# Three feed-forwards of a two-layer encoder: their first hidden group as a fifth seven-product group, and some low parts formed by adding DMAs

## The chip, the core and the metric

The kernel runs on one core of a Trainium2 chip. The core has a matmul engine (TensorE; PE on the page, its weight loads PEld), VectorE (DVE), ScalarE (ACT), GpSimd (POOL) and SyncE (SP); the engines run side by side and meet through semaphores. Matmuls read SBUF and add into eight banks of PSUM. Weights come from HBM by DMA, issued here by SP (plain loads) or by POOL (loads that add to what stands in SBUF). The metric is the device time of one execution in microseconds (us). A difference of about 0.2% (4.3 us) can be told from none in this kernel.

## The reference

512 tokens of width 1024 pass through two layers; each has a half-weight SwiGLU feed-forward, a token mixer, a cross-attention into 256 memory tokens, and a second feed-forward, each with a residual and a layer norm. All is fp32.

```python
def swiglu(x, w_gate, w_up, w_down):
    return (jax.nn.silu(x @ w_gate) * (x @ w_up)) @ w_down
...
    for i in range(DEPTH):                       # DEPTH = 2
        y = swiglu(x, ffn_w_gate[i, 0], ffn_w_up[i, 0], ffn_w_down[i, 0])
        x = layer_norm(ALPHA * x + 0.5 * y, ln_g[i, 0], ln_b[i, 0])
        y = mixer_ab(...) if i % 2 == 0 else mixer_c(...)
        x = layer_norm(ALPHA * x + y, ln_g[i, 1], ln_b[i, 1])
        y = memory_attn(x, mem, mem_w_q[i], mem_w_kv[i], mem_w_o[i])
        x = layer_norm(ALPHA * x + y, ln_g[i, 2], ln_b[i, 2])
        y = swiglu(x, ffn_w_gate[i, 1], ffn_w_up[i, 1], ffn_w_down[i, 1])
        x = layer_norm(ALPHA * x + 0.5 * y, ln_g[i, 3], ln_b[i, 3])
```

So there are four feed-forwards; gate and up are 1024 x 2816, down is 2816 x 1024. "Feed-forwards 2 to 4" are the ones with i = 1, 2, 3 in the kernel's `ffn` (line 873); the second follows the first memory attention, the third follows the second directly, the fourth is the last stage.

## The kernel before

**Precision.** Each operand is split into a high part (the value rounded to the matmul's fp32r format) and a low part (the value minus its high part). A product takes three matmuls: high by high, high by low, low by high (`mm3`, line 375). ScalarE makes the high part by a cast, VectorE the low part by a subtraction (`split`, 364; `wide`, 642, for a weight block of 128 x 1024 elements).

**Tokens.** After a layer norm each block of 128 tokens is transposed (`to_features`, 475): `xh` and `xl` hold the high and low parts with features on the partitions, and, ahead of a feed-forward, two `raw` buffers keep the unsplit values (`xf`).

**A feed-forward's hidden features** come in five groups of 512 (each two column ranges of 256, the tuple `groups`, 878) and a rest of 256. Groups 1 to 4 are made by seven products in place of eight (`hidden_steps`, 690; `quarters`, 696): the token matrix and the weight are cut into 2 x 2 quarters, sums of quarters are multiplied, and the results are added in PSUM. The products are named 1 to 7 and run in the order 1, 6, 5, 2, 7, 4, 3 for gate and then for up. Products 1, 2 and 3 use token quarters as they are (1 and 2 those of the first 256 tokens); 6, 5, 7, 4 use sums of token quarters that `token_sums` (671) makes once per feed-forward. On the weight side 1, 2 and 4 use quarters as loaded (a, b, d), 6, 5, 7, 3 sums of them; one of these sums is finished by a DMA that adds a quarter from HBM into SBUF (`plus`, 647), issued by POOL. A product is 24 matmuls of 256 columns. Product 2 adds into the bank of 1, 7 and 4 into that of 6, 3 into that of 5.

**Group 0** in feed-forwards 2 to 4 is made in full: its first 256 features by `ffn_by_tokens` (616; token blocks stationary, gate and up side by side in 512 columns, then eight transposes), its second 256 by `hidden` (658; weights stationary, all 512 tokens moving): 96 matmuls of 512 columns each. The by-token part needs one token block at a time, so it starts while later blocks are still in their layer norm.

**Down products** of group g - 1 (`down_steps`, 766) are 14 steps of six matmuls of 512 columns; `ffn` lays them between the products of group g.

**Order.** `ffn` makes a list of steps, each with a load, a preparation and a product; `staged` (862) calls the load of step j, the preparation of step j - 2 and the product of step j - 3, which fixes the order in which work is recorded. A list scheduler (`plan`, 186) then goes over all recorded operations with costs per engine, gives out buffers in the order asked for (27 weight buffers `slab` of 128 x 1024 fp32, 14 `t2`, 8 PSUM banks), and fixes each engine's order. Engines keep that order: an instruction that waits holds up those behind it on its engine. POOL's queue holds the adding DMAs, the rsqrt of the layer norms (`lny`) and some additions to x.

## Time and profile before

| | |
|---|---|
| Median of 3 runs (lowest, highest) | 2127.75 us (2125.88, 2128.41) |
| Profiled execution | span 2123.9 us, first to last instruction; the page gives no other time of it, and the median lies 3.85 us above |
| TensorE busy, weight loads busy | 2109.2 us (99%), 1871.0 us (88%) |
| VectorE, ScalarE, GpSimd busy | 1735.8 (82%), 1161.2 (55%), 287.4 us (14%) |
| Granted TensorE clock | 0.998 |
| HBM read | 259.12 MB, 124 GB/s over the span |
| Adding DMAs on POOL for gate and up | 32 of 512 KB |
| Feed-forwards on the timeline | 0 to 325, 708 to 1050, 1055 to 1390, 1779 to 2124 us |

In a row of the page stand the engine, the operation, output <- inputs by the names in the program, partitions x elements, the count, then busy us and mean ns of one, then the idle time ahead of it and what ended that. Busy TensorE time is pipelined: a matmul's own duration is longer than its spacing from the next. A merged row of the timeline gives the start of its first instruction and the time to the end of its last.

### The profile page before, as it was taken

How to read it: one execution, taken by the hardware profiler on the slowest of the kernel's cores; microseconds unless marked ns; L12 is line 12 of the kernel's file. 1: busy time of each engine (PE TensorE's matmuls, PEld its weight loads, DVE VectorE, ACT ScalarE, POOL GpSimd, SP SyncE). 2: the span in 40 equal slices, each digit the busy share in tenths (PEclk: the TensorE clock that was granted, in tenths of full speed). 3: DMA queues.
4: the chain of work that ended last, by engine and by line, in shares of the span. 5: the costliest groups of instructions: out<-in, count | busy, mean ns of one | idle time of the engine just before them, and what ended most of it. 6: DMA issues, size and time to landing. Idle time of an engine off the chain costs nothing.

```text
span 2123.9 us, 32745 instructions
## 1 busy us (share of the span) xinstructions
PE 2109.2 (99%) x12648; PEld 1871.0 (88%) x12648; DVE 1735.8 (82%) x2500; ACT 1161.2 (55%) x1903; POOL 287.4 (14%) x379
## 2 busy tenths in 40 slices
PE   9999999999999999999999999999999999999997
PEld 7999988888888899998889999888888888999996
DVE  7789988888748879998879999866577479699997
ACT  5555443698546554545545455457764465444552
POOL 0001015310102000000200000312210021000003
PEclk9999999999999999999999999999999999999999
DMA  6566562004434346564445556356454433456551
GB/s 205 141 168 144 136 191 91 21 18 116 140 125 109 90 117 181 150 158 129 148 100 143 126 139 186 78 147 165 119 165 155 139 93 96 110 149 155 143 149 60
DMA packets 208860, 275.93 MB, mean 130 GB/s; under 512 B 10688, under 2 KB 151616, under 8 KB 208704
## 3 DMA queue, kind: packets, MB, share of 16 engines
q1 hardware_dynamic: 175904, 221.14, 34.0%
q0 software_dynamic: 32512, 52.44, 14.1%
q8 instruction: 100, 1.64, 0.3%
q14 instruction: 56, 0.46, 0.1%
q10 hardware_dynamic: 288, 0.26, 0.0%
HBM read 259.12 MB, written 4.19 MB: 124 GB/s over the span
## 4 chain that ended last, share of the span: by engine, by line
PE 96%; DVE 1%; ACT 1%; DMA 1%; issue 0%; SPq 0%; DVEq 0%; ACTq 0%
PE a L157 59%; PE d L157 23%; PE t L157 15%; DVE slab L157 1%; ACT t L157 1%; DMA slab<-t 1%; DVE x L157 0%; ACT slab L157 0%; SPq L157 0%; DVE t L157 0%; DMA raw<-x_t 0%; ACT xh L157 0%; DVE mn L157 0%; DVE xl L157 0%; DVEq L1662 0%
## 5 line engine op out<-in xcount | busy, mean ns | idle before, releaser
L157 DVE TENSOR_TENSOR slab<-slab,slab 128x1024 fp32r<-128x1024 f32 (+3 forms) x638 | 727.5, 1166 | 69.5 <-ACT slab L157 39.9
L157 ACT CAST slab<-slab 128x1024 fp32r<-128x1024 f32 (+2 forms) x498 | 472.7, 983 | 341.5 <-DVE slab L157 173.2
L157 PE MATMUL a<-slab,slab 128*128 128x256 f32 (+3 forms) x2320 | 567.2, 322 | 0.7 <-DMA slab<-t 0.4
L157 PE MATMUL a<-xh,slab 128*128 128x256 f32 (+2 forms) x2480 | 559.9, 315 | 0.3 <-ACT slab L157 0.3
L157 PE MATMUL d<-slab,slab 128*128 128x512 f32 (+2 forms) x1856 | 447.0, 381 | 0.0
L157 PEld LDWEIGHTS a<-xh,slab 128*128 128x128 f32 x2480 | 416.4, 190 | 33.7 <-ACT slab L157 1.0
L157 PEld LDWEIGHTS a<-slab,slab 128*128 128x128 f32 x2320 | 409.5, 190 | 38.8 <-ACT t L157 1.3
L157 PE MATMUL a<-xl,slab 128*128 128x256 f32 (+1 forms) x1240 | 389.7, 314 | 0.0
L157 PE MATMUL a<-raw,slab 128*128 128x256 f32 x2048 | 388.9, 283 | 0.1
L157 PEld LDWEIGHTS d<-slab,slab 128*128 128x128 f32 x1856 | 329.0, 189 | 55.9 <-issue 0.2
L157 PEld LDWEIGHTS a<-raw,slab 128*128 128x128 f32 x2048 | 327.9, 192 | 5.4 <-ACT slab L157 0.5
L157 PEld LDWEIGHTS a<-xl,slab 128*128 128x128 f32 x1240 | 236.0, 190 | 18.4 <-DVE xl L157 0.4
L157 PE MATMUL t<-slab,slab 128*128 128x512 f32 (+1 forms) x840 | 209.5, 389 | 0.0
L157 DVE TENSOR_TENSOR slab<-raw,slab 128x1024 fp32r<-128x1024 f32 (+2 forms) x140 | 160.2, 1160 | 18.6 <-ACT slab L157 18.4
L157 PEld LDWEIGHTS t<-slab,slab 128*128 128x128 f32 x840 | 149.9, 189 | 26.3
L157 DVE TENSOR_TENSOR slab<-t,slab 128x512 fp32r<-128x512 f32 (+2 forms) x223 | 137.6, 638 | 16.4 <-ACT slab L157 15.9
L157 ACT CAST slab<-t 128x512 fp32r<-128x512 f32 (+2 forms) x223 | 120.9, 566 | 40.7 <-DVE t L157 13.9
L157 ACT CAST slab<-raw 128x1024 fp32r<-128x1024 f32 (+1 forms) x132 | 124.3, 971 | 27.9 <-PE a L157 8.8
L157 DVE SCALAR_TENSOR_TENSOR x<-d,x 128x512 f32<-128x512 f32 x168 | 114.7, 685 | 25.3 <-PE d L157 24.4
L157 ACT COPY t<-a 128x512 f32<-128x512 f32 (+1 forms) x116 | 63.5, 550 | 130.4 <-PE a L157 77.2
L157 POOL DMA_DIRECT2D slab<-ffn_w_down x40 | 47.7, 1193 | 310.3 <-DVE slab L157 276.3
L157 ACT ACTIVATE t<-a 128x512 f32<-128x512 f32 (+3 forms) x65 | 36.3, 559 | 89.0 <-PE a L157 89.0
(126 smaller groups left out, 2167.2 us busy)
## 6 DMA issues: line engine op xcount, KB each, us to landing
slab<-ffn_w_gate SPq DMA_DIRECT2D x80, 512.0 KB
slab<-ffn_w_up SPq DMA_DIRECT2D x80, 512.0 KB
slab<-ffn_w_down SPq DMA_DIRECT2D x80, 512.0 KB
slab<-ffn_w_down POOLq DMA_DIRECT2D x40, 512.0 KB, 5.8
raw<-mem_w_kv SPq DMA_DIRECT2D x16, 1024.0 KB
slab<-t SPq DMA_DIRECT2D x96, 128.0 KB
slab<-ffn_w_gate POOLq DMA_DIRECT2D x16, 512.0 KB, 7.8
slab<-ffn_w_up POOLq DMA_DIRECT2D x16, 512.0 KB, 6.0
```

The lines of the kernel that those rows point to most:

```text
L157: op.call = lambda: fn(*args, **kw)
```

## The change

Six things, all in the feed-forward code:

- In feed-forwards 2 to 4 group 0 becomes a seven-product group like the others; `ffn_by_tokens` goes. The first feed-forward keeps its way of making group 0.
- Groups 0 and 1 of these feed-forwards open with products 1 and 2 of gate and up of both groups, eight products that need only the first 256 tokens. Group 0's other ten products follow with no down step between, then group 1's ten with group 0's down steps spread among them. Group 1's products 1 use PSUM tag `d`, and its quarter a is loaded a second time for the later products.
- Low parts of the plain weight quarters that are not needed whole elsewhere go another way (`wide_late`): ScalarE copies the high part negated, and a DMA on POOL adds the weight from HBM. That is done for quarters b and d (products 2 and 4) in all 19 groups of all feed-forwards, and for a, b and d (1, 2, 4) in the two opening groups. (19 = 4 in the first, 5 in each other.)
- In the other groups quarter b's load and preparation stand at product 5 instead of 2, and quarter d's preparation at product 2 instead of 4.
- `token_sums` works in halves of the tokens, sums first and then splits; in feed-forwards 2 to 4 it is called at the preparation of group 0's product 6 instead of ahead of all groups.
- Some buffers are asked for later (`c22` at product 5, `h` one at a time).

By count, over the whole program: TensorE loses 576 matmuls of 512 columns and 24 transposes and gains 1008 matmuls of 256 columns. VectorE loses 72 operations of 128 x 1024 and gains some 64 of 128 x 512. ScalarE gains 88 negated copies and 14 casts of 128 x 1024, and 24 copies of 128 x 512. POOL gains 94 adding DMAs of 512 KB; SP issues 24 fewer loads of 256 KB and 18 more of 512 KB.

TensorE at the start of the second feed-forward, around the transposes of the last token block (`x3`; `t_` are PSUM banks, `a_1421` and `a_1425` banks of hidden features, `xh`, `xl` the tokens, `slab_` weight parts). Before:

```order
L157 MATMUL a_1421_1502<-slab_1416_1497,xl_3_84 128x512
L157 MATMUL a_1421_1502<-slab_1419_1500,xh_2_83 128x512
L157 MATMUL a_1421_1502<-slab_1420_1501,xh_2_83 128x512
L157 MATMUL t_1407_1488<-ident_1_78,x3_7_88 128x128 x4
L157 MATMUL a_1421_1502<-slab_1419_1500,xl_3_84 128x512
L157 MATMUL t_1408_1489<-ident_1_78,x3_7_88 128x128 x4
L157 MATMUL a_1421_1502<-slab_1419_1500,xh_2_83 128x512
L157 MATMUL a_1421_1502<-slab_1420_1501,xh_2_83 128x512
L157 MATMUL a_1421_1502<-slab_1419_1500,xl_3_84 128x512
```

Now:

```order
L157 MATMUL a_1425_1506<-xh_2_83,slab_1418_1499 128x256
L157 MATMUL a_1425_1506<-xh_2_83,slab_1417_1498 128x256
L157 MATMUL a_1425_1506<-xl_3_84,slab_1417_1498 128x256
L157 MATMUL t_1407_1488<-ident_1_78,x3_7_88 128x128 x4
L157 MATMUL a_1425_1506<-xh_2_83,slab_1418_1499 128x256
L157 MATMUL a_1425_1506<-xh_2_83,slab_1417_1498 128x256
L157 MATMUL t_1408_1489<-ident_1_78,x3_7_88 128x128 x4
L157 MATMUL a_1425_1506<-xl_3_84,slab_1417_1498 128x256
L157 MATMUL a_1425_1506<-xh_2_83,slab_1418_1499 128x256
L157 MATMUL a_1425_1506<-xh_2_83,slab_1417_1498 128x256
```

The transposes stood after 20 matmuls of 512 columns of the by-token part; they now stand after 41 of 256 columns, inside the second product (1 of up).

POOL at the same place, from the last addition of the memory stage on (`lny` are the layer norm's rsqrt, one for each token block). Before:

```order
L157 TENSOR_TENSOR x1_5_86<-x1_5_86,slab_1292_1373 128x512
L157 TENSOR_SCALAR lny_1379_1460<-var_1377_1458 128x1
L157 TENSOR_TENSOR lny_1379_1460<-lny_1379_1460,nhalf_8_89 128x1
L157 TENSOR_SCALAR lny_1390_1471<-var_1388_1469 128x1
L157 TENSOR_TENSOR lny_1390_1471<-lny_1390_1471,nhalf_8_89 128x1
L157 TENSOR_SCALAR lny_1398_1479<-var_1397_1478 128x1
L157 TENSOR_TENSOR lny_1398_1479<-lny_1398_1479,nhalf_8_89 128x1
L157 TENSOR_SCALAR lny_1406_1487<-var_1405_1486 128x1
L157 TENSOR_TENSOR lny_1406_1487<-lny_1406_1487,nhalf_8_89 128x1
L157 DMA slab_1461_1542<-ffn_w_gate 128x4x256
L157 DMA slab_1465_1546<-ffn_w_down 128x2x512
```

Now:

```order
L157 TENSOR_TENSOR x1_5_86<-x1_5_86,slab_1292_1373 128x512
L157 DMA slab_1418_1499<-ffn_w_up 128x4x256
L157 DMA slab_1414_1495<-ffn_w_gate 128x4x256
L157 DMA slab_1420_1501<-ffn_w_up 128x4x256
L157 DMA slab_1416_1497<-ffn_w_gate 128x4x256
L157 TENSOR_SCALAR lny_1379_1460<-var_1377_1458 128x1
L157 TENSOR_TENSOR lny_1379_1460<-lny_1379_1460,nhalf_8_89 128x1
L157 TENSOR_SCALAR lny_1390_1471<-var_1388_1469 128x1
L157 TENSOR_TENSOR lny_1390_1471<-lny_1390_1471,nhalf_8_89 128x1
L157 TENSOR_SCALAR lny_1398_1479<-var_1397_1478 128x1
L157 TENSOR_TENSOR lny_1398_1479<-lny_1398_1479,nhalf_8_89 128x1
L157 DMA slab_1431_1512<-ffn_w_gate 128x4x256
```

Four adding DMAs now stand ahead of the first token block's rsqrt, and one ahead of the last block's.

ScalarE, from the layer norm of the third token block (`x2`, written to `junk`) on. Before:

```order
L157 ACTIVATE junk_9_90,var_1397_1478<-x2_6_87,nmu_1396_1477 128x1024
L157 COPY raw_1380_1461<-t_1391_1472 128x4x128
L157 CAST xh_2_83<-t_1399_1480 128x4x128
L157 COPY raw_1381_1462<-t_1392_1473 128x4x128
L157 CAST xh_2_83<-t_1400_1481 128x4x128
L157 ACTIVATE junk_9_90,var_1405_1486<-x3_7_88,nmu_1404_1485 128x1024
L157 CAST slab_1436_1517<-slab_1435_1516 128x1024
L157 COPY raw_1380_1461<-t_1399_1480 128x4x128
L157 COPY raw_1381_1462<-t_1400_1481 128x4x128
L157 CAST slab_1439_1520<-slab_1438_1519 128x1024
```

Now:

```order
L157 ACTIVATE junk_9_90,var_1397_1478<-x2_6_87,nmu_1396_1477 128x1024
L157 COPY raw_1381_1462<-t_1392_1473 128x4x128
L157 CAST slab_1430_1511<-slab_1423_1504 128x1024
L157 ACTIVATE slab_1431_1512<-slab_1430_1511 128x1024
L157 CAST xh_2_83<-t_1399_1480 128x4x128
L157 CAST xh_2_83<-t_1400_1481 128x4x128
L157 CAST slab_1432_1513<-slab_1424_1505 128x1024
L157 ACTIVATE junk_9_90,var_1405_1486<-x3_7_88,nmu_1404_1485 128x1024
L157 COPY t2_1422_1503<-a_1421_1502 128x512
L157 COPY raw_1380_1461<-t_1399_1480 128x4x128
L157 ACTIVATE slab_1433_1514<-slab_1432_1513 128x1024
L157 CAST slab_1435_1516<-slab_1427_1508 128x1024
```

Between the square of `x2` and that of `x3` stood four operations on half-size tiles; now there are also two copies and a negated copy of the second opening group's weights, and more of these follow at once.

The diff, with the body of the removed function left out:

```diff
--- before.py
+++ after.py
@@ -613,26 +613,6 @@
             self.gated(banks[0][b], banks[1][b], dst=dst[:, :, b, :])
         return dst
 
-    def ffn_by_tokens(self, wg, wu, new):
-
...
     def quarter(self, w, q, c):
 
         z = self.slab(F32, (P, 4, 256))
@@ -643,6 +623,14 @@
         got = [self.slab(F32R, tuple(z.shape)) for _ in range(2)]
         self.split(z, *got)
         return got
+
+    def wide_late(self, z, w, q, c):
+
+        hi, lo = self.slab(F32R, (P, 4, 256)), self.slab(F32R, (P, 4, 256))
+        self.nc.scalar.copy(hi, z)
+        self.nc.scalar.activation(lo, hi.bitcast(F32), AF.Copy, scale=-1.0)
+        self.plus(lo, w.bitcast(F32R), q, c)
+        return [hi, lo]
 
@@ -670,30 +658,50 @@
 
     def token_sums(self):
 
-        x = [[self.xf[q][:, :, 256 * s : 256 * s + 256] for s in range(2)] for q in range(2)]
         new = lambda: self.slab(F32, (P, 4, 256))
-        t1 = self.mix(new(), x[0][0], x[0][1], ALU.subtract)
-        t2 = self.mix(new(), x[1][1], t1, ALU.add)
-        t3 = self.mix(new(), x[0][1], x[1][1], ALU.subtract)
-        t4 = self.mix(new(), x[1][0], t2, ALU.subtract)
+        t1, t2, t3, t4 = (new() for _ in range(4))
         got = {}
         for ms in ((5, 6), (7, 4)):
             room = self.tile(self.raw, [P, 2, 4, 256], F32R, "raw")
             for i, m in enumerate(ms):
-                z = {5: t1, 6: t2, 7: t3, 4: t4}[m]
                 got[m] = room[:, i], self.slab(F32R, (P, 4, 256))
-                self.split(z, *got[m])
-        for m, (q, s) in {1: (0, 0), 2: (1, 0), 3: (1, 1)}.items():
-            got[m] = [z[:, 4 * q : 4 * q + 4, 256 * s : 256 * s + 256] for z in (self.xh, self.xl)]
-        return got
-
-    def hidden_steps(self, wg, wu, c1, c2, xs, h):
+        for j in range(2):
+            at = slice(j * P, j * P + P)
+            x = [[self.xf[q][:, :, 256 * s + j * P : 256 * s + j * P + P] for s in range(2)] for q in range(2)]
+            self.mix(t1[:, :, at], x[0][0], x[0][1], ALU.subtract)
+            self.mix(t2[:, :, at], x[1][1], t1[:, :, at], ALU.add)
+            self.mix(t3[:, :, at], x[0][1], x[1][1], ALU.subtract)
+            self.mix(t4[:, :, at], x[1][0], t2[:, :, at], ALU.subtract)
+        for m, z in ((6, t2), (5, t1), (7, t3), (4, t4)):
+            for at in (slice(0, P), slice(P, 2 * P)) if m == 6 else (slice(0, 2 * P),):
+                self.split(z[:, :, at], *(y[:, :, at] for y in got[m]))
+        return {**got, **self.token_parts()}
+
+    def token_parts(self):
+
+        return {
+            m: [z[:, 4 * q : 4 * q + 4, 256 * s : 256 * s + 256] for z in (self.xh, self.xl)]
+            for m, (q, s) in {1: (0, 0), 2: (1, 0), 3: (1, 1)}.items()
+        }
+
+    def hidden_steps(self, wg, wu, c1, c2, xs, h, first=None):
 
 
         gate = {}
-        return [step for w in (wg, wu) for step in self.quarters(w, c1, c2, xs, h, gate, w is wu)]
-
-    def quarters(self, w, c1, c2, xs, h, gate, up):
+        both = [self.quarters(w, c1, c2, xs, h, gate, w is wu, first) for w in (wg, wu)]
+        order = (1, 6, 5, 2, 7, 4, 3)
+        if first is None:
+            return [steps[m] for steps in both for m in order]
+        if first == 0:
+
+            def sums():
+                xs.update(self.token_sums())
+
+            load, prep, product = both[0][6]
+            both[0][6] = load, lambda: (sums(), prep()), product
+        return [steps[m] for m in (1, 2) for steps in both] + [steps[m] for steps in both for m in order if m not in (1, 2)]
+
+    def quarters(self, w, c1, c2, xs, h, gate, up, first):
 
 
         nc, mix = self.nc, self.mix
@@ -704,9 +712,11 @@
             if m == 1:
                 raw["a"] = self.quarter(w, 0, c1)
             elif m == 6:
+                if first:
+                    raw["a"] = self.quarter(w, 0, c1)
                 raw["c"] = self.quarter(w, 0, c2)
                 raw["d"] = self.quarter(w, 1, c2)
-            elif m == 2:
+            if m == (5 if first is None else 1):
                 raw["b"] = self.quarter(w, 1, c1)
 
         def prep(m):
@@ -714,14 +724,22 @@
                 raw["v"] = mix(self.slab(F32, (P, 4, 256)), raw["a"], raw["c"], ALU.add)
                 raw["u"] = mix(raw["c"], raw["c"], raw["d"], ALU.add)
                 mix(raw["a"], raw["a"], raw["u"], ALU.add)
-            left[m] = self.wide(raw[{1: "a", 6: "a", 5: "u", 2: "b", 7: "v", 4: "d", 3: "a"}[m]])
+            if first is not None and m == 1:
+                left[1] = self.wide_late(raw["a"], w, 0, c1)
+                left[2] = self.wide_late(raw["b"], w, 1, c1)
+            if m not in left:
+                left[m] = self.wide(raw[{1: "a", 6: "a", 5: "u", 7: "v", 3: "a"}[m]])
             if m == 6:
                 self.plus(raw["a"], w, 1, c1)
+            if m == 5 and first is None:
+                left[2] = self.wide_late(raw["b"], w, 1, c1)
+            if m == (2 if first is None else 5):
+                left[4] = self.wide_late(raw["d"], w, 1, c2)
 
...
 
         def product(m):
             if m in fill:
-                own[m] = self.ps("a")
+                own[m] = self.ps("d" if first and m == 1 else "a")
             ps, wt = own[onto.get(m, m)], left.pop(m)
             for b in range(2):
                 for k in range(4):
...
@@ -756,7 +775,7 @@
                 done(int(m == 4), 0, ps)
 
         bound = lambda f, m: lambda: f(m)
-        return [tuple(bound(f, m) for f in (load, prep, product)) for m in (1, 6, 5, 2, 7, 4, 3)]
+        return {m: tuple(bound(f, m) for f in (load, prep, product)) for m in (1, 6, 5, 2, 7, 4, 3)}
 
@@ -878,11 +897,11 @@
         groups = ((0, 1024), (256, 1280), (512, 1536), (768, 1792), (2048, 2304))
         none = lambda: None
         only = lambda f: (none, none, f)
-        hs = [[] for _ in groups]
+        hs = [[None, None] for _ in groups]
         new = lambda: self.slab(F32, (P, 2, 2, 256))
-        hs[0].append((self.ffn_by_tokens if i else self.ffn_by_features)(wg, wu, new))
-        hs[0].append(self.hidden(wg, wu, groups[0][1], new))
-        xs = self.token_sums()
+        if i == 0:
+            hs[0] = [self.ffn_by_features(wg, wu, new), self.hidden(wg, wu, groups[0][1], new)]
+        xs = self.token_parts() if i else self.token_sums()
 
         def after_first():
             if aside:
@@ -890,13 +909,22 @@
                 aside()
                 nc.after = None
 
-        steps = []
+        steps, hids = [], {}
+        if i:
+            hids = {g: self.hidden_steps(wg, wu, *groups[g], xs, hs[g], g) for g in range(2)}
+            steps = hids[0][:4] + hids[1][:4] + hids[0][4:]
         for g in range(1, 5):
-            hid = self.hidden_steps(wg, wu, *groups[g], xs, hs[g])
             down = self.down_steps(hs[g - 1], wd, *groups[g - 1], coef, u2, False, i == 0 and g == 1)
-            steps += hid[:2]
-            for p, q in zip(down, hid[2:] + [None] * 2):
-                steps += [p, q] if q else [p]
+            if g in hids:
+                hid = hids[g][4:]
+                for k, q in enumerate(hid):
+                    lo, hi = (len(down) * z // len(hid) for z in (k, k + 1))
+                    steps += [q] + down[lo:hi]
+            else:
+                hid = self.hidden_steps(wg, wu, *groups[g], xs, hs[g])
+                steps += hid[:2]
+                for p, q in zip(down, hid[2:] + [None] * 2):
+                    steps += [p, q] if q else [p]
             if g == 1:
                 steps.append(only(after_first))
```

24 lines of the change are left out of this document (4 added, 20 removed).

## The prediction

> **What bounds the kernel now.** I read the page's totals first, then the chain that ended last, then the list of what TensorE waited for.
>
> ```profile
> span 2123.9 us, 32745 instructions
> PE 2109.2 (99%) x12648; PEld 1871.0 (88%) x12648; DVE 1735.8 (82%) x2500; ACT 1161.2 (55%) x1903; POOL 287.4 (14%) x379
> q0 software_dynamic: 32512, 52.44, 14.1%
> PE 96%; DVE 1%; ACT 1%; DMA 1%; issue 0%; SPq 0%; DVEq 0%; ACTq 0%
> PE t L157 <- DVE junk L157: 1.2, 1, 1.2
> PE t L157 <- DVE x L157: 0.7, 1, 0.7
> PE t L157 <- DVE slab L157: 0.4, 1, 0.4
> PE a L157 <- DMA slab<-t: 0.4, 2, 0.2
> PE a L157 <- DVE slab L157: 0.4, 1, 0.4
> PE a L157 <- ACT slab L157: 0.3, 1, 0.3
> ```
>
> The last six rows are the whole wait list of TensorE: 3.4 us, of which 1.2 us is the start. The chain is TensorE for 96% of the span. A busy TensorE is only pipelined, so the share alone proves nothing; the wait list does: the kernel is as long as its matmuls' spacing makes it. A matmul taken out is worth its spacing, unless something new makes TensorE wait. Both are to be priced.
>
> Spacing, from two stretches of the second feed-forward on the timeline (start, duration, then the operation):
>
> ```profile
> 759.29 1.55 PE L157 MATMUL d<-slab,slab 128*128 128x512 f32 x6
> 763.55 0.63 PE L157 MATMUL d<-slab,slab 128*128 128x512 f32 x2
> ...
> 729.70 0.39 PE L157 MATMUL d<-slab,xh 128*128 128x512 f32 x1
> 730.84 0.82 PE L157 MATMUL t<-ident,t 128*128 128x128 f32 x6
> 731.41 0.48 PE L157 MATMUL a<-xh,slab 128*128 128x512 f32 x1
> 731.73 0.40 PE L157 MATMUL a<-xl,slab 128*128 128x512 f32 x1
> 732.20 0.38 PE L157 MATMUL t<-ident,t 128*128 128x128 f32 x2
> 732.33 0.47 PE L157 MATMUL a<-xh,slab 128*128 128x512 f32 x1
> ```
>
> Between 729.70 and 730.84 start five matmuls of 512 columns: 0.228 us each. Between 759.29 and 763.55 lie six of 512 and one product, 24 of 256 columns: (4.26 - 6 x 0.228) / 24 = 0.1205 us each. Two of 256 cost 0.241, 6% more than one of 512. The eight transposes of the by-token group take 0.57 (six) and 0.13 (two), and the 512-column matmul behind each batch starts its successor 0.09 late (0.32 instead of 0.228, at 731.41 to 731.73): 0.88 us together.
>
> **The change on TensorE.** For feed-forwards 2 to 4 the counts of the built kernels differ by -576 matmuls of 512 columns (192 each: 96 by tokens, 96 by features), +1008 of 256 (336 each: two matrices, seven products, 24 each), -24 transposes. Outside the feed-forwards TensorE's order is the same. So -576 x 0.228 = -131.3, +1008 x 0.1205 = +121.5, -3 x 0.88 = -2.6: **-12.4 us**. All of it lies on the path that sets the end. That is a ceiling: with 3.4 us of waits there is next to nothing else to win.
>
> A rule speaks against this. The Trainium skill, "TensorE: Matmul & The Clock Gate", section "Back-to-back issue gap", gives real streams as about 81 ns a matmul at 128 columns and 131 ns at 512. An estimate half way, some 97 ns at 256, would make the sum 1008 x 0.097 - 576 x 0.131 = +22 us, so slower. The trace disagrees: 228 ns at 512 and 120 ns at 256 are this kernel's own streams, weight loads included.
>
> **What preparation costs beside it.** These rows price it (mean ns in the first four; the last two are KB each and us from issue to landing):
>
> ```profile
> L157 DVE TENSOR_TENSOR slab<-slab,slab 128x1024 fp32r<-128x1024 f32 x422 | 516.1, 1233 | 59.9 <-ACT slab L157 39.1 <-PE a L157 16.1 <-PE t L157 2.1
> L157 ACT CAST slab<-slab 128x1024 fp32r<-128x1024 f32 x422 | 435.1, 1050 | 332.8 <-DVE slab L157 171.0 <-PE a L157 101.1 <-DMA slab<-ffn_w_up 31.5
> L157 DVE TENSOR_TENSOR t<-a,t 128x512 f32<-128x512 f32 x72 | 49.5, 687 | 11.7 <-PE a L157 11.3
> L157 POOL DMA_DIRECT2D slab<-ffn_w_gate x16 | 21.1, 1319 | 419.6 <-DVE slab L157 353.0 <-DMA slab<-ffn_w_gate 28.0 <-issue 25.8
> slab<-ffn_w_gate POOLq DMA_DIRECT2D x16, 512.0 KB, 7.8
> slab<-ffn_w_up POOLq DMA_DIRECT2D x16, 512.0 KB, 6.0
> ```
>
> 88 low parts leave VectorE's subtraction (1.233 each) for a negated copy on ScalarE (not in the trace; the nearest row is the cast, 1.05) and an adding DMA (1.3 on POOL, landed after 6.0 to 7.8); six more adding DMAs come with the new groups. VectorE gains and loses other work: 72 fewer operations of 1024 elements, some 64 more of 512: about -45 us of 1735.8, all beside TensorE, worth 0 to the end, since TensorE waits 0.8 us for VectorE's tiles after the start. ScalarE's +115 us or so (88 + 14 at 1.05, the rest copies) takes it to 60%: no bound either. A low part comes some 6 us later than by subtraction (7.8 + 1.05 against 1.233, at worst 7.6).
>
> In the steady groups I take 0 for that. Cover and its limit (mean groups of the second feed-forward, busy us by engine, clock, DMA share, GB/s; then ScalarE's waits):
>
> ```profile
> 813.00:872.00 59.00, 59.00 (x419) 55.53 (x418) 54.78 (x65) 30.48 (x38) 4.94 (x4) 1.00 0.60 152
> ACT slab L157 <- PE a L157: 196.9, 94, 7.6
> ```
>
> ScalarE opens each weight's preparation, and it stands 94 times waiting for TensorE to give a buffer back: preparation runs a buffer's turn ahead. And the code prepares part 2 one product and one down step earlier than before (2.9 + 1.4 = 4.3 us), part 4 two of each (8.6 us). If that cover were gone: 52 such parts at up to 7.6 us, hundreds of us; nothing in the row suggests it. Four more adding DMAs a group raise its 152 GB/s to about 188, and the share by 4 x 3.0 / 59 = 0.20 to 0.80 (3.0 us: 14.1% of the span over 100 half-megabyte transfers). That is the thinner cover.
>
> **The openings are where it can be lost.** Each of the three now begins with eight plain products, all with low parts by DMA, 24 x 0.1205 = 2.89 us each, 23.1 together; then ten products with no down step between. What stands there now:
>
> ```profile
> 691.66 0.18 POOL L157 TENSOR_SCALAR lny<-var 128x1 f32<-128x1 f32 x1 [5.22 <-ACT junk L157]
> 702.07 0.37 SPq L157 DMA_DIRECT2D slab<-ffn_w_gate  x1
> 705.12 0.92 SPq L157 DMA_DIRECT2D slab<-ffn_w_up  x2
> 708.13 0.62 PE L157 MATMUL a<-slab,xh 128*128 128x512 f32 x2
> 709.38 1.15 ACT L157 ACTIVATE junk<-x,nmu 128x1024 bf16<-128x1024 f32 x1 [0.39 <-DVE nmu L157]
> 711.72 1.40 DVE L157 SCALAR_TENSOR_TENSOR x<-slab,lny,slab 128x512 f32<-128x512 f32 x2
> 707.50:753.00 45.50, 45.50 (x212) 37.82 (x212) 33.66 (x39) 23.33 (x33) 2.12 (x3) 1.00 0.39 111
> ```
>
> The feed-forward starts at 708.1, and weight buffers beyond the first dozen come free only at 702 to 708. The first group's four low parts are issued on POOL ahead of the first token block's rsqrt: four times 1.3 us where POOL idles 5.2 us, so that block slips by about a microsecond, under the down products of three others. The second group's loads start at about 705, and ScalarE then has, up to its fourth negated copy, eight weight operations (8.4), one square (1.3) and five half-size ones (0.6 each): 12.7 us, so 718. Landed 7.8 later: 726. TensorE wants that part after seven products and the last block's transposes (0.9): 708.1 + 0.9 + 20.2 = 729.2. The first needs 720.6 and has 716; the two between have 2 to 3 us. The token sums must be split before the ninth product, 732: the last block's rows leave VectorE at about 713, and fifteen operations of 0.7 to 1.2 us and the copies they wait on end near 728. Everything is in time, but by 2 to 4 us, where the old opening had VectorE 74% busy and no wait. ScalarE's square of the last block stands behind two new weight copies: it slips about 0.7 us, and the transposes behind it have 41 short matmuls as cover (4.9 us) instead of 20 long ones (4.6). I take **1.2 us** of new waits per opening, 3.6 in all, nearer the lower end because every step computed is early. Bounds: nothing below 0, since the products themselves are counted; above, if the second group's four transfers follow one another at 7.8 us, the last lands at 708 + 31 = 739, 10 us late, three times: +30.
>
> Sum against the profiled span: 2123.9 - 12.4 + 3.6 = 2115.1. The median of the three runs shown, 2127.75, stands 3.85 above that span; kept, it gives **2119.0 us**, 0.4% faster (2115.4 if the openings cost nothing).
>
> **Rivals.** (1) Half the gain goes. The ten products without down steps ask VectorE for 35 us (token sums and splits 10.6, weights 2 x 7 x 1.233, banks 10 x 0.69) within some 48, in an order TensorE follows at once; if it is 2 to 4 us late in each opening, 2121.5 to 2127. For it: VectorE at 54.78 of 59 in steady groups shows how dense such stretches get. Against: that density costs TensorE nothing there. (2) Slower: low parts late at the opening's second group. The place is the queue of adding DMAs, and the point is the rate: four must land within some 21 us of 708. At 3.0 us each (queue 0's mean share) they are early; at 5.3 they begin to cost; beyond 6.4 each opening loses over 4.1 us, its whole gain; at 7.8, 10 us each: 2127.75 - 12.4 + 30 = 2145. The 7.8 is a time from issue to landing with its start in it, measured while loads ran beside it, so consecutive ones should overlap. (3) Slower in the steady groups: with the DMA share at 0.8, loads come late; a microsecond and a half in each of 13 groups is +20, 2135. The Trainium skill, "DMA: Bandwidth & Descriptors", section "Issuing engines are not separate DMA queues", says that all queues share the same 16 engines, and the 7.8 against 6.0 above agrees. Against it: the buffer waits just quoted. (4) Slower, short matmuls bound by their weight loads: 432 more loads (the page's loads keep their unit busy 88% of the span). At 0.131 us per short matmul the gain is gone, at a load's mean of 1871.0 / 12648 = 0.148 it is 1008 x 0.0275 = +28, 2143. Against it: the short matmuls of the stretches above come at 0.1205 with their loads. This is what the TensorE page's rule would amount to. That the change does not do what it says is left out: the counts above are those of the built kernels.
>
> **Numbers.** Gain mostly kept, 2114 to 2121.5: 0.62. Rival 1: 0.20. Rivals 2, 3 and 4: 0.08, 0.05 and 0.01. A full gain with something more, below 2114: 0.04. The range that leaves out at most 2 in 10 runs from 2113 to 2130; the forecast's own is 2114 to 2121.5. This kernel tells about 0.2%, 4.3 us, from no change: below 2123.5 lie 0.62, 0.04 and somewhat over half of rival 1, 0.78; above 2132 most of rivals 2 to 4, 0.10; the rest, 0.12, is no difference.
>
> **What would show it.** Right: 512-column matmuls fewer by 576, spacings of 0.228 and 0.120 unchanged, TensorE's wait list under 8 us, the stretch from the second feed-forward's first product to its 16th of group one without a gap over 1 us, steady groups at 59 to 60 us. Rival 1: waits of TensorE for VectorE's tiles or ScalarE's in those ten products. Rival 2: TensorE waiting for a DMA into a weight buffer 12 to 25 us after each feed-forward's start. Rival 3: steady groups over 61 us, and ScalarE waiting more for loads and less for TensorE. The forecast is wrong if TensorE's waits grow by more than 8 us, or if 256-column matmuls come at more than 0.125 us.

## The result: slower by 1%

The changed kernel takes 2148.26 us (median of 4 runs) where the kernel before takes 2127.59: the ratio is 1.0102, with a 95% interval of 1.0088 to 1.0117. The forecast was 2119. The page of the changed kernel, in the rows that answer to those shown before:

```profile
span 2144.9 us, 33922 instructions
PE 2107.5 (98%) x13056; PEld 1888.2 (88%) x13056; DVE 1688.0 (79%) x2480; ACT 1268.3 (59%) x2019; POOL 403.6 (19%) x473
q1 hardware_dynamic: 178880, 224.28, 33.0%
q0 software_dynamic: 82144, 101.73, 28.4%
PE 81%; DMA 6%; DVE 5%; ACT 4%; issue 2%; POOL 1%; SPq 0%; DVEq 0%; ACTq 0%; POOLq 0%
```

The span grew by 21.0 us, and TensorE's share of the chain that ended last fell from 96% to 81%. Its list of waits (total us, times, longest) shows where; the whole list went from 3.4 to 26.0 us:

```profile
PE a L157 <- DVE t L157: 18.8, 11, 3.1
PE t L157 <- DVE x L157: 2.7, 6, 1.0
PE t L157 <- DVE junk L157: 1.2, 1, 1.2
```

The spacing of matmuls did not change. In a stretch of the second feed-forward without waits (start, duration, operation):

```profile
782.05 2.91 PE L157 MATMUL t<-slab,slab 128*128 128x512 f32 x12
784.80 0.28 PE L157 MATMUL a<-raw,slab 128*128 128x256 f32 x1
...
787.67 1.55 PE L157 MATMUL d<-slab,slab 128*128 128x512 f32 x6
```

Twelve of 512 columns in 2.75 us are 0.229 each, then 24 of 256 in 2.87 are 0.1196 each. So the 12.4 us forecast from the counts and these spacings were won. I then took the start of every matmul to the start of the next, less its normal spacing, and summed: 25.1 us of excess before, 58.2 now, 33.1 more. 33.1 - 12.4 = 20.7 against the measured 21.0, so the account closes. The 33.1 us are:

| Excess over before | us |
|---|---|
| Ten waits of 1.0 to 3.3 us in the 13 steady groups | 19.9 |
| Four stretches after such waits at a lower granted clock | 6.5 |
| Waits in the three openings | 4.7 |
| One wait behind the third feed-forward's end | 1.1 |
| Smaller ones | 0.9 |

**What one of the ten waits is.** These rows are of the second feed-forward's group 4, its last (a down quarter is a quarter of the weight block of a group's down products; four are loaded, the last two of them named 22 and 21), from the timelines of POOL, SP, ScalarE, VectorE and TensorE (in brackets the idle time before, and what ended it):

```profile
938.72 1.28 POOL L157 DMA_DIRECT2D slab<-ffn_w_gate  x1 [23.49 <-DVE slab L157]
941.66 1.28 POOL L157 DMA_DIRECT2D slab<-ffn_w_gate  x1 [1.66 <-ACT slab L157]
944.26 1.28 POOL L157 DMA_DIRECT2D slab<-ffn_w_gate  x1 [1.32 <-ACT slab L157]
945.01 1.75 POOL L157 DMA_DIRECT2D slab<-ffn_w_down  x1
951.04 1.20 POOL L157 DMA_DIRECT2D slab<-ffn_w_down  x1 [4.28 <-DVE slab L157]
...
952.51 0.37 SPq L157 DMA_DIRECT2D slab<-ffn_w_down  x1
...
959.79 1.05 ACT L157 CAST slab<-slab 128x1024 fp32r<-128x1024 f32 x1 [5.62 <-DMA slab<-ffn_w_down]
960.87 1.22 DVE L157 TENSOR_TENSOR slab<-slab,slab 128x1024 fp32r<-128x1024 f32 x1 [4.25 <-ACT slab L157]
963.74 0.69 DVE L157 TENSOR_TENSOR t<-a,t 128x512 f32<-128x512 f32 x1
...
964.48 0.39 PE L157 MATMUL a<-raw,slab 128*128 128x256 f32 x1 [1.83 <-DVE t L157]
```

Read from the end. TensorE's product 4 adds into a bank that VectorE must read first (963.74). VectorE's queue is in order, and ahead of that read stands the subtraction for a down quarter (960.87), which waits for ScalarE's cast (959.79), which waits 5.62 us for that quarter's load. SP issued the load at 952.51, 10.7 us after the group's first product began (941.85), when VectorE gave a buffer back; in the kernel before it was issued 3.1 us after it (935.47 against 932.41). And when it was issued, the 16 DMA engines were still at the last two of five adding transfers in a row, which landed at 954.96 and 958.08 (busy us of the engines, clock, DMA share, GB/s; the share adds up the packets' times, so it passes 1.00 where packets overlap):

```profile
936.00:938.00 2.00, 2.00 (x17) 1.95 (x16) 1.77 (x3) 2.00 (x3) 0.00 (x0) 1.00 0.00 0
938.00:940.00 2.00, 2.00 (x15) 1.86 (x14) 2.00 (x4) 0.98 (x2) 1.28 (x1) 1.00 0.03 8
...
946.00:948.00 2.00, 2.00 (x17) 1.96 (x16) 0.82 (x1) 0.00 (x0) 0.76 (x1) 1.00 1.10 182
948.00:950.00 2.00, 2.00 (x15) 1.78 (x14) 2.00 (x4) 1.56 (x3) 0.00 (x0) 1.00 1.24 197
950.00:952.00 2.00, 2.00 (x18) 2.00 (x18) 2.00 (x3) 1.44 (x3) 0.96 (x1) 1.00 1.24 204
952.00:954.00 2.00, 2.00 (x14) 1.75 (x13) 2.00 (x4) 1.93 (x3) 0.24 (x1) 1.00 1.13 206
954.00:956.00 2.00, 2.00 (x19) 2.00 (x18) 2.00 (x4) 0.17 (x1) 0.00 (x0) 1.00 1.13 207
956.00:958.00 2.00, 2.00 (x14) 1.74 (x13) 0.62 (x1) 0.00 (x0) 0.00 (x0) 1.00 1.06 337
```

The engines stand empty from about 933 to 940, are full from 942 on, and move some 205 GB/s while they add but 337 when plain loads run again. Over the whole kernel ScalarE's list of waits has a row that the kernel before has not, while its wait for TensorE's buffers fell from 196.9 to 160.7 us:

```profile
ACT slab L157 <- PE a L157: 160.7, 69, 5.5
...
ACT slab L157 <- DMA slab<-ffn_w_down: 67.1, 19, 5.7
```

### The profile page after: what moved, and what is told of

It is laid out like the page before. It is cut to its first block, busy times and chain, and to the rows that moved or that the text cites. A ratio compares the mean times of both kernels' runs of the same rounds, so it can differ in the third digit from the quotient of the medians.

```text
span 2144.9 us, 33922 instructions
## 1 busy us (share of the span) xinstructions
PE 2107.5 (98%) x13056; PEld 1888.2 (88%) x13056; DVE 1688.0 (79%) x2480; ACT 1268.3 (59%) x2019; POOL 403.6 (19%) x473
## 3 DMA queue, kind: packets, MB, share of 16 engines
q0 software_dynamic: 82144, 101.73, 28.4%
## 4 chain that ended last, share of the span: by engine, by line
PE 81%; DMA 6%; DVE 5%; ACT 4%; issue 2%; POOL 1%; SPq 0%; DVEq 0%; ACTq 0%; POOLq 0%
PE a L157 49%; PE d L157 19%; PE t L157 13%; DMA slab<-ffn_w_down 5%; DVE slab L157 4%; ACT slab L157 2%; ACT t L157 1%; DVE x L157 1%; DVE t L157 1%; DMA slab<-ffn_w_up 1%; POOL slab L157 1%; ACT raw L157 0%; DMA slab<-t 0%; DMA slab<-ffn_w_gate 0%; ACT xh L157 0%
## 5 line engine op out<-in xcount | busy, mean ns | idle before, releaser
L157 DVE TENSOR_TENSOR slab<-slab,slab 128x1024 fp32r<-128x1024 f32 (+3 forms) x586 | 666.7, 1161 | 125.8 <-ACT slab L157 87.5
L157 ACT CAST slab<-slab 128x1024 fp32r<-128x1024 f32 (+2 forms) x516 | 493.8, 984 | 348.2 <-DVE slab L157 124.8
L157 PE MATMUL a<-slab,slab 128*128 128x256 f32 (+2 forms) x2512 | 624.3, 321 | 0.8 <-DMA slab<-t 0.6
L157 PE MATMUL a<-xh,slab 128*128 128x256 f32 (+2 forms) x2384 | 517.9, 307 | 0.5 <-ACT slab L157 0.5
L157 PE MATMUL a<-raw,slab 128*128 128x256 f32 x2432 | 466.9, 286 | 19.6 <-DVE t L157 18.8
L157 PEld LDWEIGHTS a<-slab,slab 128*128 128x128 f32 x2512 | 449.1, 191 | 38.5 <-ACT t L157 1.3
L157 PEld LDWEIGHTS a<-raw,slab 128*128 128x128 f32 x2432 | 393.3, 194 | 28.4 <-DVE t L157 22.8
L157 PE MATMUL a<-xl,slab 128*128 128x256 f32 (+2 forms) x1192 | 366.6, 308 | 0.0
L157 DVE TENSOR_TENSOR slab<-raw,slab 128x1024 fp32r<-128x1024 f32 (+2 forms) x148 | 160.7, 1105 | 20.0 <-ACT slab L157 19.9
L157 POOL DMA_DIRECT2D slab<-ffn_w_gate x63 | 83.3, 1327 | 411.6 <-DVE slab L157 343.9
L157 POOL DMA_DIRECT2D slab<-ffn_w_up x63 | 81.2, 1337 | 361.3 <-PE a L157 141.5
```

The lines of the kernel that those rows point to most:

```text
L157: op.call = lambda: fn(*args, **kw)
```

## The experiments

Two theories. A: the change prepares parts 2 and 4 earlier, so their buffers are taken earlier, and the rotation hands the down quarters theirs late. B: the adding transfers fill the DMA engines. Ratios below are to the kernel before, run beside each set (medians 2126.15 to 2127.08 us), with 95% intervals. For each version the scheduler plans every engine's order anew, unless the text says that the order was kept.

**The steady groups as before, the new openings kept.**

```diff
-            if m == (5 if first is None else 1):
+            if m == (2 if first is None else 1):
                 raw["b"] = self.quarter(w, 1, c1)
-            if m == 5 and first is None:
-                left[2] = self.wide_late(raw["b"], w, 1, c1)
-            if m == (2 if first is None else 5):
+            if m == 5 and first is not None:
                 left[4] = self.wide_late(raw["d"], w, 1, c2)
```

(and products 2 and 4 back in `wide`'s table)

> The new openings, with the steady groups as before: part 2 loaded and prepared at product 2, part 4 at product 4, both low parts by subtraction. Both theories place the loss in the steady groups, where TensorE stands about 2 us for a VectorE bank read (10 times, plus about 1.5 us of lower granted clock after some of them): here that wait should be gone, TensorE's wait list under 10 us, and the sum 2123.9 - 12.4 + 3 to 6 stand: span 2114 to 2118, median 2117 to 2122. If the median stays over 2135, the loss comes from the openings or from the token sums.

2122.66 us, ratio 0.9977 (0.9967 to 0.9986), span 2120.8. The loss is in the steady groups; the fifth seven-product group, its openings' low parts still by adding DMAs, is faster by 4.4 us, a third of its 12.4. Excess over normal spacing is 34.1 us, 9.0 more than before, and 9.0 - 12.4 = -3.4 against a span shorter by 3.1. Of the 9.0, 6.4 are waits in the three openings.

**Subtraction in the steady groups, at the change's early places.**

```diff
-                left[2] = self.wide_late(raw["b"], w, 1, c1)
+                left[2] = self.wide(raw["b"])
...
-                left[4] = self.wide_late(raw["d"], w, 1, c2)
+                left[4] = self.wide(raw["d"])
```

> The changed kernel, but in the steady groups parts 2 and 4 get their low parts by subtraction, at the same early places as in the change. Theory A (buffers: the pairs for parts 2 and 4 are taken one or two products earlier, so the rotation of 27 buffers hands the down quarters theirs later): the waits for VectorE's bank read stay, 2140 to 2150. Theory B (transfers: five adding DMAs in a row hold the engines that the down quarter's load and the next adding DMA need): the waits go, 2116 to 2122.

2125.46 us, ratio 0.9991 (0.9982 to 1.0000). The wait for the bank read falls from 18.8 us to 2.7:

```profile
PE t L157 <- DVE x L157: 4.4, 5, 1.8
PE a L157 <- DVE t L157: 2.7, 3, 1.2
```

The early places alone are not the cause: theory A as stated falls. The time lies 3.5 us above what theory B gave, so the early places may cost a little of their own.

**Adding DMAs at the old places.**

```diff
-            if m == 5 and first is None:
+            if m == 2 and first is None:
                 left[2] = self.wide_late(raw["b"], w, 1, c1)
-            if m == (2 if first is None else 5):
+            if m == (4 if first is None else 5):
                 left[4] = self.wide_late(raw["d"], w, 1, c2)
```

(with quarter b's load at product 2)

> The changed kernel, but in the steady groups parts 2 and 4 are loaded and prepared at the old places (products 2 and 4), still with adding DMAs. Theory A (buffers): the pairs are taken late again, the down quarter's load is issued early, 2116 to 2125. Theory B (transfers): as many adding DMAs, the down quarter still late or other waits in its place, 2135 to 2150.

2156.76 us, ratio 1.0138 (1.0123 to 1.0154). Later places are worse, beyond either theory's range: besides 14.8 us for the bank read, TensorE now waits 11.2 us for the parts' own transfers, which it never does in the change. That is what the early places are good for.

**The steady groups' part of the change alone, in the kernel before.** (The same lines of `prep` and `load`, and `wide_late`, put into the kernel before.)

> The kernel before with the steady groups' part of the change alone: parts 2 and 4 of groups 1 to 4 by a negated copy and an adding DMA, at the change's earlier places; group 0 as before. If the steady groups alone cause the loss, 12 to 16 groups wait 1 to 3 us each and some run a few microseconds at a lower clock: 2127.6 + 20 to 40, so 2147 to 2167. If the loss needs the new openings too, 2126 to 2132.

2160.88 us, ratio 1.0161 (1.0147 to 1.0175). It needs nothing of the new openings:

```profile
PE a L157 <- DVE t L157: 20.3, 11, 2.6
```

**The same transfers, but overwriting; and without them.** The order of every engine is that of the changed kernel.

```diff
         self.nc.scalar.activation(lo, hi.bitcast(F32), AF.Copy, scale=-1.0)
-        self.plus(lo, w.bitcast(F32R), q, c)
+        self.nc.gpsimd.dma_start(out=lo, in_=w.bitcast(F32R)[512 * q : 512 * q + 512, c : c + 256].rearrange("(k p) f -> p k f", p=P))
```

(without `accum_op`; two lines that make the scheduler plan the transfer like an adding one are not shown; in the second of the two runs the transfer is left out)

> The changed kernel with every engine's order kept, but the 88 added low-part DMAs on POOL overwrite instead of add (those low parts are then wrong: the negated copy is lost). POOL's issues, ScalarE's copies, the buffers and the bytes read stay. Theory B as time of the 16 engines (an adding transfer holds them about 2.8 us, a plain one about half): most of the waits go, 2118 to 2130. Theory B as place in POOL's queue, or as latency from issue to landing: the waits stay, 2140 to 2150.

2124.94 us, ratio 0.9995 (0.9986 to 1.0005). The wait for the bank read falls from 18.8 us to 5.4, in the same order of every engine:

```profile
PE a L157 <- DVE t L157: 5.4, 5, 3.0
```

In the group shown above SP issues the down quarter as late as in the change, 9.7 us after the group's first product (945.04 against 935.35). But it has landed 5.6 us after its issue instead of 7.2, so 15.3 us after that product instead of 17.9; ScalarE's cast still waits for it, and TensorE does not wait:

```profile
950.68 1.05 ACT L157 CAST slab<-slab 128x1024 fp32r<-128x1024 f32 x1 [3.06 <-DMA slab<-ffn_w_down]
```

So the late issue alone costs nothing here.

> The changed kernel with every engine's order kept, but the 88 added low-part DMAs are left out (those low parts are then only the negated high part). ScalarE's negated copies, the buffers and the places of the steps stay. If the transfers cause the loss: 2114 to 2122, with only the openings' waits left. If ScalarE's added copies or the fixed order (planned for slow transfers) cause it: 2135 to 2150.

2119.89 us, ratio 0.9970 (0.9957 to 0.9982). So neither ScalarE's 88 copies nor the order cost anything, and POOL's 88 issues with plain transfers cost 5 us: the 23.3 us between the change and the overwriting version (22.8 by the ratios) are the adding itself. POOL's queue in these two (packets, MB, share of 16 engines):

```profile
q0 software_dynamic: 82144, 101.73, 24.1%
```

```profile
q0 software_dynamic: 35680, 55.58, 15.0%
```

Against 15.0% of 2118.8 us without them, the packets of the 88 transfers take 28.4% of 2144.9 less that, 291 us of the 16 engines' time, 3.3 us each, where they add; 24.1% of 2121.1 less that, 193 us, 2.2 us each, where they overwrite.

**The late down quarter loaded earlier.**

```diff
                 fetch("22")
-            elif m == 2:
                 fetch("21")
```

> The changed kernel, but the fourth down quarter (21) is loaded together with the third (22), two products earlier. In the change the last link of each 2 us wait is this quarter: issued some 10 us after the group's first product begins, behind the adding DMAs on the 16 engines. If its own lateness is the link, the waits shrink to under 10 us in all, 2120 to 2132. If the adding DMAs delay whatever stands beside them (then the next adding DMA, into the sum that product 4 uses, or another load), 2138 to 2150.

2157.79 us, ratio 1.0154 (1.0139 to 1.0168). Asking for it earlier moves the load but not the lateness: the bank read costs 27.5 us in 12 waits. In the group shown above the quarter is now issued at 945.03, as the group's first product begins (945.07), and the second adding DMA into the down sums lands 10.7 us after its issue, against 7.0 in the change. (The profiled execution, 2163.61 us, was the slowest of the four.) What stands behind the adding transfers is late, whichever it is.

**Half of the adding DMAs.**

> The changed kernel, but in the steady groups only part 2 (quarter b) gets its low part by an adding DMA; part 4 is subtracted, at the change's place. That is 26 of the 52 adding DMAs of the steady groups. If each costs the same, half of the 23 us between the changed kernel and its subtracting twin (2125.5) goes: 2135 to 2139. If it is the row of them, one behind another beside the down quarters' loads, the row is one shorter and most of the loss goes: 2124 to 2132.

> The other half: in the steady groups only part 4 (quarter d) by an adding DMA, part 2 subtracted. By number: 2135 to 2139, like the run with part 2 alone. By the row: 2124 to 2132; and as part 4's transfer is the last of the row ahead of the down sum's, it should leave more of the loss than part 2's does.

2123.14 us, ratio 0.9984 (0.9975 to 0.9993), and 2122.07, ratio 0.9975 (0.9966 to 0.9985). Either half costs nothing. That is below what either reading gave: the cost is not in proportion to the number, and part 4's transfers leave no more of the loss than part 2's. The cast that waited 5.62 us waits 0.49 where only part 4 is added:

```profile
946.49 1.05 ACT L157 CAST slab<-slab 128x1024 fp32r<-128x1024 f32 x1 [0.49 <-DMA slab<-ffn_w_down]
```

**All of them, but part 4's set apart.**

```diff
-            if m == (2 if first is None else 5):
+            if m == (7 if first is None else 5):
                 left[4] = self.wide_late(raw["d"], w, 1, c2)
```

> The changed kernel with all 52 adding DMAs in the steady groups, but part 4 is prepared one product later (at product 7 instead of 2), so that its transfer stands apart from part 2's and from the down sums'. If the row (one stretch of 15 us or more with the 16 engines full) is what costs: stretches under 10 us, and 2120 to 2130. If the number of transfers in a group costs (mean DMA share near 0.8), wherever they stand: 2140 to 2160, as in the run with both parts at their old places (2156.8).

2149.98 us, ratio 1.0110 (1.0096 to 1.0124). In the group shown the row of five is now three, a pause and two (POOL issues at 934.11, 937.05 and 939.74, then at 947.62 and 948.35), yet the waits stay, 19.0 us for the bank read. So one unbroken row is not needed, and the number is what is left; but part 4's transfer now goes out right behind the second one into the down sums, so the edit did not set it apart from these as intended. The three steady groups of the second feed-forward, each from its first product to the next group's, give a bound (the last two numbers are DMA share and GB/s), the change first, then the version with part 4 alone, then the overwriting one:

```profile
818.70:878.30 59.60, 59.60 (x421) 56.07 (x420) 52.03 (x63) 34.04 (x43) 10.08 (x9) 1.00 0.81 187
878.30:941.85 63.55, 61.63 (x421) 57.47 (x420) 50.76 (x61) 34.28 (x43) 10.11 (x9) 0.97 0.73 167
941.85:1003.99 62.14, 60.31 (x422) 56.14 (x421) 50.95 (x62) 34.79 (x43) 9.83 (x8) 1.00 0.81 202
```

```profile
811.71:871.31 59.60, 59.60 (x421) 56.04 (x420) 54.33 (x65) 32.38 (x41) 7.51 (x6) 1.00 0.70 168
871.31:930.93 59.62, 59.62 (x421) 56.05 (x420) 52.91 (x63) 32.62 (x41) 7.57 (x6) 1.00 0.66 160
930.93:990.55 59.62, 59.62 (x421) 56.05 (x420) 53.59 (x64) 32.46 (x41) 7.45 (x6) 1.00 0.74 193
```

```profile
815.28:874.88 59.60, 59.60 (x421) 56.04 (x420) 52.47 (x63) 34.12 (x43) 8.00 (x9) 1.00 0.72 184
874.88:935.35 60.47, 59.87 (x421) 55.95 (x420) 50.58 (x61) 34.29 (x43) 8.04 (x9) 1.00 0.70 176
935.35:994.97 59.62, 59.62 (x422) 56.04 (x421) 50.88 (x62) 34.75 (x43) 7.76 (x8) 1.00 0.77 210
```

Share times length, as a mean over three groups: 48.3 us of the engines' time a group in the change, 41.7 and 43.7 in the two that lose nothing. Of a group of 59.6 us that is 0.81 against 0.70 and 0.73. But the mean does not decide for a single group: the first of the change's three has 48.3 us and no wait, the second 46.4 and a wait of 2.1 us.

**More and fewer weight buffers.**

```diff
-    BUFS = {"t2": 14, "slab": 27, ...}
+    BUFS = {"t2": 12, "slab": 28, ...}
```

> The changed kernel with 28 weight buffers in place of 27 (and 12 of the small buffers in place of 14, to make room). The 16 DMA engines stand idle in parts of each half group and are full in others, since a load is issued only when a buffer comes free. If that lead is what turns 26 more adding DMAs into waits, one buffer more lets loads run about one product earlier and takes at least a third of the 23 us: under 2141. If the engines' time alone is short, it stays at 2144 to 2152.

> Control for the run with 28 buffers: the changed kernel with 12 small buffers in place of 14 and its 27 weight buffers. 2146 to 2152 if the small buffers don't matter; over 2155 if they do.

> The run with part 4 alone by adding DMA (2122.1), with 26 weight buffers in place of 27. If 26 adding DMAs cost nothing because the loads still run far enough ahead, one buffer less brings back waits of the kind seen in the change: over 2130. If half the number is simply within what the engines can do: 2120 to 2126.

With 28 weight buffers 2141.97 us, ratio 1.0072 (1.0057 to 1.0087); the control with 27, 2153.15, ratio 1.0126 (1.0109 to 1.0143); part 4 alone with 26, 2125.37, ratio 0.9997 (0.9987 to 1.0006); this last version also orders buffers that come free at the same moment in another way, so the missing buffer is not its only edit. First the row with 28, then the control's:

```profile
PE a L157 <- DVE t L157: 11.7, 10, 2.2
```

```profile
PE a L157 <- DVE t L157: 20.6, 12, 3.2
```

One buffer more takes 11.2 us off its control, more than a third of the loss, though the bound I had written (under 2141) was missed by 1. The control itself lies between its two forecasts, 4.9 us above the change, so the small buffers count too; against the change the version with 28 is 6.3 us faster. One fewer costs the half version 3.3 us, not the 8 that a return of the waits would have cost. So the lead that free buffers give to loads appears to be part of the mechanism, but it does not alone set the point at which waits begin.

**The openings.** With the steady groups as before:

```diff
+            late = self.wide_late if first == 0 else lambda z, *_: self.wide(z)
-                left[1] = self.wide_late(raw["a"], w, 0, c1)
+                left[1] = late(raw["a"], w, 0, c1)
```

(and the same for parts 2 and 4; `first == 1` in the third of the three runs; in the first of them `wide_late` itself subtracts)

> No low part by DMA at all: steady groups as before, and the openings' parts a, b, d by subtraction too. The version with subtraction in the steady groups alone had 8.5 us of waits more than before, 6.4 us of them in the three openings, where a negated copy on ScalarE and an adding DMA on POOL stand ahead of a layer norm's square and rsqrt. If these are what delays the transposes: 3 to 5 us off, 2117 to 2120. If VectorE, with some 10 more subtractions in each opening, becomes what is waited for: 2122 to 2130.

> Steady groups as before; in the openings only the first group's six low parts by adding DMA, the second group's subtracted. With all twelve by DMA the median was 2122.7, with all subtracted 2126.4. If in the all-DMA version the second group's negated copies and adding DMAs hold up the layer norm's square and rsqrt, and in the all-subtracted one VectorE's work for the first group is what is late, this takes the better of both: 2117 to 2121. If the costs just add: about 2124 to 2125.

> Steady groups as before; in the openings only the second group's six low parts by adding DMA, the first group's subtracted. By the first theory of the run before (the second group's copies hold up the layer norm, the first group's subtractions load VectorE at its densest): 2123 to 2128. If VectorE is densest after the last layer norm, while the second group and the token sums are prepared: 2117 to 2121.

All subtracted: 2126.39 us, ratio 1.0002 (0.9993 to 1.0011). The first group's by DMA: 2123.33, 0.9985 (0.9976 to 0.9994). The second group's by DMA: 2118.77, 0.9959 (0.9947 to 0.9972). The last is a version faster than both kernels; its TensorE waits 5.9 us in all:

```profile
PE t L157 <- DVE x L157: 2.0, 2, 1.3
PE t L157 <- DVE junk L157: 1.2, 1, 1.2
PE a L157 <- DVE slab L157: 0.7, 2, 0.4
```

My first reading, that the second group's copies and DMAs hold up the layer norms, is contradicted: those are the ones worth having. The changed kernel does show such holds (in the third feed-forward's opening a square of the layer norm stands behind a negated copy, and a rsqrt behind an adding DMA), and the all-subtracted version has a wait of 3.5 us for ScalarE in the second feed-forward's first down products. But with each edit the scheduler lays the whole opening anew, so which of these the 4 to 8 us belong to stays open.

**The best opening with the half that costs nothing.**

> The two best single choices together: in the openings only the second group's low parts by adding DMA (2118.8 alone), in the steady groups only part 4's (2122.1 with the change's openings, where plain subtraction had 2122.7). If they are independent, the steady part's adding DMAs are worth nothing either way: 2117 to 2120. If the freed VectorE time helps the steady groups: below 2117. If even 26 adding DMAs cost something that the openings' waits hid: 2120 to 2125.

2118.61 us, ratio 0.9964 (0.9950 to 0.9977): the same as without. The steady groups' adding DMAs are worth nothing where they fit and 23 us where they don't, since the VectorE time that they free is not on the path there. In the openings the choice matters: from 2126.4 us with none to 2118.8 with the second group's.

## Why the prediction was wrong

**Right: the counts and the spacing.** The -12.4 us on TensorE came out within what the account can tell (20.7 against 21.0), with spacings of 0.229 and 0.1196. The rule of the Trainium skill that spoke against it ("TensorE: Matmul & The Clock Gate", section "Back-to-back issue gap") would have made these counts +22 us, by chance the size of the loss; the trace disagrees, and the account shows that it is not where the loss came from. Rival 4 falls with it.

**Nearly right: the openings.** 3.6 us of new waits were taken for the three; 4.7 were measured. TensorE waits for no weight transfer there, and in the second feed-forward no gap from the first product to the 16th is over 0.5 us. The second group's fourth low part was forecast 18 us after the start against a need at 21.1; issued at 726.99, it landed 11.5 us later, 21.5 after the start (717.01), and its product began after 21.8. Rival 2 did not happen, with 0.3 us to spare, so that the openings came out well was partly luck.

**Wrong: "In the steady groups I take 0 for that".** This is the step that failed: waits and lower clock cost 26.4 us in 13 groups. Of the forecast's miss in the span (2144.9 - 2115.1 = 29.8), 26.4 are this, 1.1 the openings, 1.1 the wait behind the third feed-forward, 0.9 smaller ones. The prediction had the resource in hand: it worked out 3.0 us for an adding transfer (measured 3.3) and a share of 0.80 (measured 0.81 of the old length), and called it "the thinner cover". Three readings went wrong after that.

- I took a mean share below 1 for room. Loads are issued as buffers come free, so the engines stand empty at 934 to 940 and full after 942; the delay at the full places counts, not the mean alone.
- I asked only whether the moved low parts would be late. They are not: TensorE never waits for them in the changed kernel. Late is what shares the engines with them, the down quarters and the down sums' own adding DMAs, and they hold ScalarE and VectorE, whose queues then hold a bank read.
- "ScalarE stands 94 times waiting for TensorE to give a buffer back: preparation runs a buffer's turn ahead" served as the argument against rival 3. The same row says that buffers are scarce, so that loads cannot be issued earlier when transfers get slower. The run with one buffer more speaks for that: 11.2 us against its control.

Rival 3 was thus the right case with a chance of 0.05; its price, a microsecond and a half a group or +20, was near the measured 26.4 us, and its signs came as written: two of the three groups shown take 62.1 and 63.6 us, by way of the bank read, and ScalarE waits more for loads and less for TensorE. The rule named beside it (the Trainium skill, "DMA: Bandwidth & Descriptors", section "Issuing engines are not separate DMA queues": all queues end on the same 16 engines) is what the runs show: transfers issued by POOL make loads issued by SP late.

Two small ones. Of the 3.85 us between span and median about half was the spread of runs: the changed kernel's profiled run took 2146.66 us for a span of 2144.9, so 1.8 lie around the span. And the wait list before shows 1.5 us for VectorE's tiles after the start (0.7, 0.4, 0.4), not 0.8; nothing hung on it.

**Open.** That adding instead of overwriting costs the 23 us is shown, with every engine's order kept. Why 42 to 44 us of the engines' time a group cost nothing and 48 cost 2 us of waits is known only as a bound between runs; the buffers seem to be part of it, and the order in which the scheduler lays the transfers may be another.

## What to carry to other kernels

Before moving work from an idle-looking engine's subtraction to the DMA engines, look at who else uses these in the same microseconds and how far ahead loads can be issued with the buffers there are; a mean share of 0.8 with scarce buffers can already be too full. An adding transfer is dearer than the same one that overwrites, here by half. And test the parts of a change apart: without any of the new adding DMAs the group change was worth nothing, with those of its openings 4 us, with the best choice of them 8, while in the steady groups the same DMAs gave nothing and cost 23.

## What the hardware did that I had not expected

**A short stop can cost twice.** After four of the ten waits the granted TensorE clock fell to 0.50 for 3.41 us; matmuls of 256 columns then came every 0.213 us instead of 0.120, 1.6 us more each time. Around the wait at 898.7, and around the one at 962, which was as long (2.1 us) and had no such stretch (the third number from the end is the granted clock):

```profile
898.43:901.84 3.41, 1.49 (x8) 0.99 (x8) 3.41 (x5) 2.56 (x4) 0.00 (x0) 1.00 0.78 230
901.84:905.25 3.41, 3.41 (x18) 3.41 (x17) 3.38 (x4) 0.00 (x0) 0.00 (x0) 0.50 0.02 5
905.25:908.66 3.41, 3.41 (x26) 3.25 (x26) 2.13 (x4) 2.48 (x3) 0.00 (x0) 1.00 0.00 0
959.87:963.28 3.41, 2.78 (x14) 1.83 (x12) 2.41 (x3) 3.41 (x5) 0.00 (x0) 1.00 0.85 256
963.28:966.69 3.41, 2.21 (x18) 2.21 (x19) 3.41 (x5) 1.18 (x3) 0.00 (x0) 1.00 0.46 150
```

It depends on where the stop falls. The four low stretches start at 256.72, 901.84, 1246.58 and 2041.89 us, 189, 101 and 233 times 3.413 us apart, so they lie on one fixed grid. In the grid's stretch just ahead of each, TensorE was busy 1.49 to 1.65 us of 3.41. The wait at 962 is cut by a boundary of the grid: 2.78 and 2.21 us busy on its two sides, and the clock stayed. Two other stretches with about 1.7 us busy had no low clock behind them, so in this run the limit lies near there. The Trainium skill, "TensorE: Matmul & The Clock Gate", section "Part 1: The HAM clock gate", describes a half-rate state set by activity in windows of about 3.4 us that run freely; the trace agrees in the length and in the grid.

**Adding against overwriting.** The packets of the same 512 KB, from the same queue, took 3.3 us of the 16 engines' time where they were added and 2.2 us where they overwrote.
